# HGRN heads of a decoder trunk: the output norm in two halves, the last late projection's finish behind the keys' copies, and two weight sums of the feed-forward passage moved back

## The chip, the cores and the metric

The kernel runs on one core of a Trainium2 chip. The metric is the device time of one execution in microseconds (us); the median of several runs is compared. Where the text gives positions ("at 511 us"), they are counted from the start of the span of the profiled execution.

## What is computed

One layer of an autoregressive decoder, sequence 1024, width 1024, batch 1, all in fp32:

```
h <- h + W_out [ HGRN2 | dilated-window attention mixture | RWKV-7 ](W_in rmsnorm(h))
h <- h + gated MLP (width 2816) with causal depthwise conv (width 3) on rmsnorm(h)
h <- h + sigmoid(rmsnorm(h) W_g) * (p W_p)
...
final RMSNorm
```

The change is in the HGRN2 part (four heads, key and value width 128) and in the first half of the MLP. Of HGRN2, the part that matters here is its end, after the recurrence `S_t = diag(f_t) S_{t-1} + (1 - f_t) i_t^T, o_t = S_t^T q_t`:

```
o = o * lax.rsqrt(jnp.mean(o * o, axis=-1, keepdims=True) + NORM_EPS)      # per position and head, over 128
o = o.reshape(B_, S_, HG_WIDTH) * gnorm_g * jax.nn.silu(g_raw)
```

## The kernel before

Every dense product of fp32 numbers is made of three products of rounded parts: x = xh + xl, w = whi + wlo, and xh whi + xl whi + xh wlo is summed in PSUM (lines L137, L139, L141). ScalarE (ACT) makes the high parts, whi at L114 and xh at L160; VectorE (DVE) or GpSimd (POOL) makes the low parts, wlo at L116 and xl at L162. TensorE is PE.

The phases are: norm of x; RWKV with most of the projections by W_in; then the stretch that this change touches, from about 430 to 570 us: the four HGRN heads, the window attention, the last projections by W_in and the first tiles of W_out; then the rest of W_out, the MLP, the per-layer input and the final norm.

The stretch is written as generators that are advanced in turn by an order string: `A` is head 0 and then head 2, `B` head 1 and then head 3, `C` the attention (`swa`), `F` the late projections (`project_late`, in the order ... 18, 22, 23). Each `yield` is a place where another generator goes on. A scheduler then puts the instructions of every engine in one order. `tc.issue_after(x)` tells it that what is written inside must come later in the order than x; it adds no wait of its own.

One head, `hgrn_head`, goes: gates and decays on VectorE and GpSimd (names zl, hT, hk, qt); scores of chunks (hsc, masked into hS); transposes of the values (PE `vt`, L1043, copied to `hV` by ACT, L1044) and of the keys (`vt`, L1049, copied to `hkt` by ACT, L1050); the states (`hkv` in PSUM, `hst`); the outputs (`hpo`, L1083 and L1085). Then comes its end, L1086 to L1104: ACT copies the two halves of the output to `ho` (hf = 0 and then hf = 1, 128x512 each); ACT squares all of it (`hsq`, 128x1024); VectorE sums the squares by position (`hss`, 128x8) and applies mean and epsilon; GpSimd raises to -1/2 (`hrs`, 128x8); VectorE multiplies `ho` by it (L1097); PE transposes the two halves (`vt`, L1103); and VectorE multiplies by gain and gate (L1104). `o_split` then makes the two parts of the result for the product with W_out, whose PSUM tiles are `dp`.

In `project_late`, each projection is made in two halves of 128x512 (PSUM tile `zp`), and each half is finished at once: VectorE scales it (L320), ACT takes the sigmoid (`zst`, L457), VectorE multiplies (L459), and the queue of SP stores it to DRAM (L477), from where a head loads it back (`zl`, L488). For the last one, 23, this is the gate of head 3.

PSUM: a pool of four banks of 128x512 (`mx`) serves zp, vt, hsc, hkv, hpo and attention's tiles (swt, swo, swd) in turn. Attention's scores are `swq`; its probabilities lg, transposed by PE into swt and copied to pT.

In the first half of the MLP, weights and activations are combined by a seven-product scheme (p1 to p7) in the "passage" over the first units, at about 655 to 690 us. `sums` makes sums of weights of a unit on VectorE (L1448, L1450, L1451). The `y` of a unit is the last sum into V (L1510); PE writes into that PSUM tile again after it.

Of the kernel before, what the change touches and what calls it, by code (L numbers as in the profile page):

```python
# [22 lines left out]
NFF = 22  # L23
EPS = 1e-6
# [5 lines left out]
PC_LB, PC_GN, PC_MU = 32, 36, 40  # L30
# [59 lines left out]
class Trunk:  # L90
# [370 lines left out]
    def project_late(self, js):  # L461


        nc = self.nc
        for j in js:
            w = self.load_w(self.a["w_in"][j])
            t = self.keep.tile([P, T], F32, tag="zst", name=self.nm("zst"), bufs=2)
            d = self.zpool.tile([P, T], F32, tag=f"z{j}", name=f"z{j}")
            kind = (j - 8) % 4 if j < 24 else 2
            turn = j < 24 and kind < 3  # L470
            for hf in (0, 1):
                ps = self.mxp.tile([P, HT], F32, tag="mx", name=self.nm("zp"))
                self.dense({hf: ps}, w, self.X, ND, halves=(hf,))
                dst = slice((hf ^ turn) * HT, ((hf ^ turn) + 1) * HT)
                r = self.R[:, hf * HT:(hf + 1) * HT]
                self.finish(kind, t[:, dst], *((ps[:, ::-1], r[:, ::-1]) if turn and hf else (ps, r)))
                nc.sync.dma_start(d[:, dst], t[:, dst])  # L477
                if hf:
                    self.z[j] = d
                yield  # L480
        self.O = self.xall()
        for k in self.done:
            self.o_split(k)
            yield
# [469 lines left out]
    def hgrn_head(self, h):  # L954
        nc, mxp, par, spool = self.nc, self.mxp, self.par, self.spool
        j0 = 8 + 4 * h

        def view(t, off, *dims):
            return bass.AP(t.tensor, t.offset + off, [t.ap[0], *dims])

        f = self.zload(j0, self.slot)
# [77 lines left out]
        V = self.slot("hV")  # L1039
        for hf in (0, 1):  # L1040
            pt = mxp.tile([P, HT], F32, tag="mx", name=self.nm("vt"))
# [3 lines left out]
        kt = self.slot("hkt")  # L1045
        for hf in (0, 1):
            pt = mxp.tile([P, HT], F32, tag="mx", name=self.nm("vt"))
            for c in range(4):
                nc.tensor.transpose(pt[:, c * P:(c + 1) * P], k[:, hf * HT + c * P:hf * HT + (c + 1) * P], self.ident)  # L1049
            nc.scalar.copy(kt[:, hf * HT:(hf + 1) * HT], pt)  # L1050
        yield
        st = self.slot("hst")

        def at(cc, swap=False):
            c = (4 + cc if cc < 4 else 7 - cc) ^ (4 if swap else 0)
            return slice(c * P, (c + 1) * P)

        for hf in (0, 1):
# [6 lines left out]
            for c in range(4):  # L1065
# [3 lines left out]
                dst = st[:, (cc + 1) * P:(cc + 2) * P]  # L1069
# [5 lines left out]
                                                   ALU.mult, ALU.add)  # L1075
        yield
        o = self.slot("ho")
        for hf in (0, 1):
            po = mxp.tile([P, 4, P], F32, tag="mx", name=self.nm("hpo"))
            for c in range(4):  # L1080
                cc = 7 - c if hf == 0 else c
                s = at(cc)
                nc.tensor.matmul(po[:, c, :], S[:, s], V[:, s], start=True, stop=cc == 0)  # L1083
                if cc:
                    nc.tensor.matmul(po[:, c, :], qt[:, s], st[:, cc * P:(cc + 1) * P], start=False, stop=True)  # L1085
            nc.scalar.copy(o[:, hf * HT:(hf + 1) * HT], po.rearrange("p c v -> p (c v)"))  # L1086
        yield
        oa = self.zload(j0 + 3, self.slot)
        sq = self.slot("hsq")
        nc.scalar.activation(sq, o, AF.Square)  # L1090
        ss = spool.tile([P, 8], F32, tag="hss", name=self.nm("hss"))
        nc.vector.tensor_reduce(ss, sq.rearrange("p (c v) -> p c v", v=P), AX.X, ALU.add)
        nc.vector.tensor_scalar(ss, ss, 1.0 / P, EPS, ALU.mult, ALU.add)
        rs = spool.tile([P, 8], F32, tag="hrs", name=self.nm("hrs"))
        nc.gpsimd.tensor_tensor(rs, ss, self.mhalf[:, :8], ALU.pow)
        o3 = o.rearrange("p (c v) -> p c v", v=P)
        nc.vector.tensor_tensor(o3, o3, rs.unsqueeze(2).broadcast_to([P, 8, P]), ALU.mult)  # L1097
        yield
        for hf in (0, 1):
            sl = slice((1 - hf) * HT, (2 - hf) * HT)  # L1100
            pt = mxp.tile([P, HT], F32, tag="mx", name=self.nm("vt"))
            for c in range(4):
                nc.tensor.transpose(pt[:, c * P:(c + 1) * P], o3[:, hf * 4 + c, :], self.ident)  # L1103
            nc.vector.scalar_tensor_tensor(oa[:, sl], pt if hf else pt[:, ::-1], par[:, PC_GN + h:PC_GN + h + 1], oa[:, sl], ALU.mult, ALU.mult)  # L1104
        self.o[h] = oa
        self.dump(f"o{h}", oa)
        self.o_split(h)
# [324 lines left out]
    def phase_up(self):  # L1432
        nc, par, ep, cv, TX = self.nc, self.par, self.ep, self.cv, self.TX
        V, G = nc.vector, nc.gpsimd
# [9 lines left out]
        def sums(d):  # L1444
            a11, a12 = d["raw"][:, :HT], d["raw"][:, HT:]
            a21, a22 = d["rav"][:, :HT], d["rav"][:, HT:]
            s7 = ep.tile([P, HT], F32, tag="s7", name=self.nm("s7"), bufs=1)
            V.tensor_tensor(s7, a11, a21, ALU.add)  # L1448
            s6 = ep.tile([P, HT], F32, tag="s6", name=self.nm("s6"), bufs=2)
            V.tensor_tensor(s6, s7, a22, ALU.add)  # L1450
            V.tensor_tensor(a21, a21, a22, ALU.add)  # L1451
            d["s"] = {"3": s6, "4": a22, "5": a21, "6": s6, "7": s7, "2": a12}

        def w(d, n):
# [7 lines left out]
        def unit(d, prev):  # L1462
            f = d["f"]
# [8 lines left out]
            if prev:  # L1472
                ws["4"] = w(prev, "4")
            sums(d)
            for n in "652" if new else "65":
                ws[n] = w(d, n)
# [30 lines left out]
            x = cv.tile([P, HT], F32, tag="x", name=self.nm("x"), bufs=1)  # L1507
            d["x"] = V.tensor_tensor(x, d["e"], d["G"][:, HT:], ALU.add).ins
            self.mul((d["V"][:, :HT], ws["7"], TX["p7"], False))
            V.tensor_tensor(d["V"][:, HT:], x, d["V"][:, :HT], ALU.add)  # L1510

        def conv(d, part):
            f = d["f"]
# [35 lines left out]
        for d in self.units:  # L1549
            unit(d, prev)  # L1550
            prev = d
# [308 lines left out]
```

## Time and profile before

| | |
|---|---|
| median of 3 runs | 1404.72 us (1404.64 to 1406.29) |
| profiled execution: time | 1404.77 us |
| its span | 1403.0 us |
| mean granted clock of TensorE | 0.994 |
| PE busy | 1375.7 us, 98% of the span |
| DVE, ACT, POOL busy | 76%, 44%, 28% |

An entry of the profile such as `511.21 1.06 PE L1049 MATMUL vt<-cst,hk ... x4 [2.44 <-ACT hV L1044]` means: at 511.21 us four transposes that write vt began on TensorE; the engine had stood still for 2.44 us before, until ACT's instruction that writes hV, line 1044, was done. Line numbers are those of the kernel before; behind `issue_after` and the new code they are five to sixteen higher in the kernel after.

### The profile page before, as it was taken

Reading aid. Unit: us, or ns where it says so; the run is one execution under the profiler, and the core shown is the slowest. Engines: PE = TensorE matmul, PEld = TensorE weight load, DVE = VectorE, ACT = ScalarE, POOL = GpSimd, SP = SyncE. Lnnn points to the kernel's source line nnn. Section 1 sums busy time; section 2 is a strip of 40 time slices with the busy share of each in tenths; the row PEclk is TensorE's granted clock in tenths of the full one; section 3 lists DMA queues with packets and bytes.
Section 4 is the critical chain, followed back from the end, with each engine's and each line's share of the span. In section 5 each row is a group of like instructions: output and inputs, shape, how many; then the busy total and the mean of one; then the engine's idle time right before and its main releaser. Section 6 shows DMA issues by size and latency. Waiting matters only on the chain.

```text
span 1403.0 us, 22344 instructions
## 1 busy us (share of the span) xinstructions
PE 1375.7 (98%) x8644; PEld 1116.5 (80%) x8644; DVE 1063.7 (76%) x1613; ACT 611.8 (44%) x1049; POOL 395.5 (28%) x287
## 2 busy tenths in 40 slices
PE   9999999999999999999999999999999999999997
PEld 6878777877878768788788888888888888888886
DVE  7696456835667796468889888888988799777685
ACT  7522323133255584255544343444344444455542
POOL 5411012101222242221345454545453000002342
PEclk9999999999999999999999999999999999999998
DMA  6123111321622212653232332332324963441443
GB/s 224 61 83 104 64 61 47 100 73 62 225 83 99 91 61 71 253 180 125 94 127 98 113 103 90 102 105 98 114 98 166 351 217 106 127 143 45 136 138 140
DMA packets 80122, 167.61 MB, mean 119 GB/s; under 512 B 19984, under 2 KB 22288, under 8 KB 80016
## 3 DMA queue, kind: packets, MB, share of 16 engines
q1 hardware_dynamic: 66784, 147.05, 31.3%
q10 hardware_dynamic: 12224, 15.47, 3.2%
q0 software_dynamic: 1008, 3.67, 0.7%
q8 instruction: 68, 1.11, 0.3%
q14 instruction: 38, 0.31, 0.1%
HBM read 119.76 MB, written 46.40 MB: 118 GB/s over the span
## 4 chain that ended last, share of the span: by engine, by line
PE 78%; DVE 8%; issue 8%; ACT 3%; POOL 3%; DMA 1%; SPq 0%; POOLq 0%; ACTq 0%; DVEq 0%
PE bg L1338 17%; PE bv L1338 13%; PE bv L1639 7%; PE bg L1639 7%; PE dp L137 7%; PE dp L139 7%; PE dp L141 7%; PE swq L1169 1%; DVE ig L584 1%; PE hsc L1015 1%; PE zp L137 1%; DVE xl L409 1%; PE zp L141 1%; PE zp L139 1%; PE swo L1209 1%
## 5 line engine op out<-in xcount | busy, mean ns | idle before, releaser
L137 PE MATMUL dp<-xh,whi 128*128 128x512 f32 x544 | 186.9, 406 | 1.2 <-DVE r L502 0.7
L139 PE MATMUL dp<-xl,whi 128*128 128x512 f32 x544 | 180.5, 394 | 0.6 <-DVE xl L409 0.5
L141 PE MATMUL dp<-xh,wlo 128*128 128x512 f32 x544 | 179.7, 392 | 0.0
L116 POOL TENSOR_TENSOR wlo<-wraw,whi 128x512 fp32r<-128x512 f32 x60 | 84.5, 1410 | 264.9 <-ACT whi L114 226.8
L116 POOL TENSOR_TENSOR wlo<-raw,whi 128x512 fp32r<-128x512 f32 x84 | 135.0, 1626 | 75.9 <-ACT whi L114 75.9
L114 ACT CAST whi<-wraw 128x512 fp32r<-128x512 f32 x120 | 72.9, 618 | 158.0 <-PE dp L139 103.0
L1338 PE MATMUL bg<-t,whi 128*128 128x512 f32 x352 | 133.4, 389 | 0.0
L139 PEld LDWEIGHTS dp<-xl,whi 128*128 128x128 f32 x544 | 102.3, 188 | 24.6 <-DVE xl L409 2.5
L141 PEld LDWEIGHTS dp<-xh,wlo 128*128 128x128 f32 x544 | 102.2, 188 | 23.8 <-issue 2.0
L137 PEld LDWEIGHTS dp<-xh,whi 128*128 128x128 f32 x544 | 98.8, 189 | 26.0 <-issue 3.9
L116 POOL TENSOR_TENSOR wlo<-s,whi 128x512 fp32r<-128x512 f32 x44 | 64.5, 1466 | 168.6 <-ACT whi L114 168.6
L1639 PE MATMUL bg<-t,whi 128*128 128x512 f32 x308 | 95.2, 390 | 0.0
L1639 PE MATMUL bv<-t,whi 128*128 128x512 f32 x308 | 94.8, 389 | 0.0
L114 ACT CAST whi<-raw 128x512 fp32r<-128x512 f32 x88 | 52.7, 620 | 93.7 <-issue 48.5
L114 ACT CAST whi<-s 128x512 fp32r<-128x512 f32 x66 | 38.9, 620 | 120.2 <-PE bg L1338 112.8
L1338 PEld LDWEIGHTS bg<-t,whi 128*128 128x128 f32 x352 | 66.1, 188 | 13.7
L190 POOL TENSOR_TENSOR rst<-rst,mhalf 128x4 f32<-128x4 f32 (+1 forms) x9 | 10.2, 1134 | 234.0 <-DVE rst L186 218.0
L1635 ACT CAST t<-t 128x512 fp32r<-128x512 f32 x77 | 47.8, 622 | 45.8 <-PE bv L1639 32.7
L1338 PE MATMUL bg<-t,wlo 128*128 128x512 f32 x176 | 67.5, 389 | 0.0
L1639 PEld LDWEIGHTS bv<-t,whi 128*128 128x128 f32 x308 | 57.8, 188 | 12.0
L1639 PEld LDWEIGHTS bg<-t,whi 128*128 128x128 f32 x308 | 57.8, 188 | 11.9
L116 DVE TENSOR_TENSOR wlo<-wraw,whi 128x512 fp32r<-128x512 f32 x60 | 48.2, 807 | 20.7 <-ACT whi L114 18.5
(417 smaller groups left out, 3423.6 us busy)
## 6 DMA issues: line engine op xcount, KB each, us to landing
raw<-in_ffn_up_dram SPq DMA_DIRECT2D x44, 512.0 KB, 3.5
wraw<-in_w_in_dram SPq DMA_DIRECT2D x28, 512.0 KB, 3.4
z<-zst SPq DMA_DIRECT2D x18, 512.0 KB, 2.9
gb<-ct SPq DMA_DIRECT2D x33, 256.0 KB, 2.3
t<-gb SPq DMA_DIRECT2D x33, 256.0 KB, 2.7
t<-gt SPq DMA_DIRECT2D x33, 256.0 KB, 2.7
zl<-z SPq DMA_DIRECT2D x16, 512.0 KB, 4.4
wraw<-in_ple_gate_dram SPq DMA_DIRECT2D x16, 512.0 KB, 3.4
```

The source lines that it names most:

```text
L114: self.cast = nc.scalar.copy(hi, src).ins
L116: eng.tensor_tensor(lo, src, hi.bitcast(F32), ALU.subtract)
L137: nc.tensor.matmul(ps[hf], wh, xh[hf], start=first, stop=False)
L139: nc.tensor.matmul(ps[hf], wh, xl[hf], start=False, stop=False)
L141: self.step = nc.tensor.matmul(ps[hf], wl, xh[hf], start=False, stop=last).ins
L409: nc.vector.scalar_tensor_tensor(lo, x, g[:, k:k + 1], hi.bitcast(F32), ALU.mult, ALU.subtract)
L584: nc.vector.reciprocal(ig[:, hf * HT:(hf + 1) * HT], gam[:, hf * HT:(hf + 1) * HT])
L1015: nc.tensor.matmul(sc[g:g + 64, c, :], ks[:, c * P + g:c * P + g + 64], x, start=True, stop=True)
L1169: m = nc.tensor.matmul(pq[h][:, b:b + w], d["q"][hs, qb * P:nk], d["k"][hs, b:b + w], start=True, stop=True)
L1338: nc.tensor.matmul(ps, w[part == 2][:, s], X[k][part == 1], start=start and k == part == 0, stop=k == 3 and part == 2, skip_group_check=no ...
L1635: nc.scalar.copy(xh, x)
L1639: nc.tensor.matmul(ps[m], wt[part == 2][:, m * P:(m + 1) * P], (xh, xl)[part == 1], start=k == part == 0, stop=k == NK - 1 and part == 2)
```

## The change

1. `project_late`: the second half of the last projection (23) is finished behind a `yield`, and in the order behind the copies of the keys of a head (`self.keys`).
2. `hgrn_head`: the output halves are made in the order hf = 1, hf = 0. Each half is copied, squared, summed, and raised to -1/2 by itself; the copy of the second half comes behind the square of the first. Both multiplies (128x512 each) come behind the second half's mean; the multiplies by gain and gate come behind both.
3. `sums` of the MLP: for unit 2, two of the three sums come behind the y of unit 0.

Per head this is one ACT instruction more, three VectorE instructions and one GpSimd instruction more. No matmul and no transfer is added.

```
@@ project_late
                 r = self.R[:, hf * HT:(hf + 1) * HT]
-                self.finish(kind, t[:, dst], ...)
+                with ExitStack() as order:
+                    if hf and j == js[-1]:
+                        yield
+                        order.enter_context(self.tc.issue_after(self.keys))
+                    self.finish(kind, t[:, dst], ...)
                 nc.sync.dma_start(d[:, dst], t[:, dst])
                 if hf:
                     self.z[j] = d
-                yield
+                if not (hf and j == js[-1]):
+                    yield
@@ hgrn_head
-            nc.scalar.copy(kt[:, hf * HT:(hf + 1) * HT], pt)
+            self.keys = nc.scalar.copy(kt[:, hf * HT:(hf + 1) * HT], pt).ins
...
-        for hf in (0, 1):
+        squared = None
+        for hf in (1, 0):
             po = mxp.tile([P, 4, P], F32, tag="mx", name=self.nm("hpo"))
...
-            nc.scalar.copy(o[:, hf * HT:(hf + 1) * HT], po.rearrange("p c v -> p (c v)"))
-        yield
-        oa = self.zload(j0 + 3, self.slot)
-        sq = self.slot("hsq")
-        nc.scalar.activation(sq, o, AF.Square)
-        ss = spool.tile([P, 8], F32, tag="hss", name=self.nm("hss"))
-        nc.vector.tensor_reduce(ss, sq.rearrange("p (c v) -> p c v", v=P), AX.X, ALU.add)
-        nc.vector.tensor_scalar(ss, ss, 1.0 / P, EPS, ALU.mult, ALU.add)
-        rs = spool.tile([P, 8], F32, tag="hrs", name=self.nm("hrs"))
-        nc.gpsimd.tensor_tensor(rs, ss, self.mhalf[:, :8], ALU.pow)
-        o3 = o.rearrange("p (c v) -> p c v", v=P)
-        nc.vector.tensor_tensor(o3, o3, rs.unsqueeze(2).broadcast_to([P, 8, P]), ALU.mult)
-        yield
-        for hf in (0, 1):
+            s, c = slice(hf * HT, (hf + 1) * HT), slice(4 * hf, 4 * hf + 4)
+            if hf:
+                oa = self.zload(j0 + 3, self.slot)
+                sq = self.slot("hsq")
+                ss, rs = [spool.tile([P, 8], F32, tag=n, name=self.nm(n)) for n in ("hss", "hrs")]
+                o3 = o.rearrange("p (c v) -> p c v", v=P)
+            with ExitStack() as order:
+                if squared is not None:
+                    order.enter_context(self.tc.issue_after(squared))
+                nc.scalar.copy(o[:, s], po.rearrange("p c v -> p (c v)"))
+            squared = nc.scalar.activation(sq[:, s], o[:, s], AF.Square).ins
+            nc.vector.tensor_reduce(ss[:, c], sq[:, s].rearrange("p (c v) -> p c v", v=P), AX.X, ALU.add)
+            m = nc.vector.tensor_scalar(ss[:, c], ss[:, c], 1.0 / P, EPS, ALU.mult, ALU.add)
+            nc.gpsimd.tensor_tensor(rs[:, c], ss[:, c], self.mhalf[:, :4], ALU.pow)
+        yield
+        with self.tc.issue_after(m.ins):
+            for c in (slice(4, 8), slice(0, 4)):
+                m = nc.vector.tensor_tensor(o3[:, c], o3[:, c], rs[:, c].unsqueeze(2).broadcast_to([P, 4, P]), ALU.mult)
+        yield
+        for hf in (1, 0):
...
-            nc.vector.scalar_tensor_tensor(oa[:, sl], ...)
+            with self.tc.issue_after(m.ins):
+                nc.vector.scalar_tensor_tensor(oa[:, sl], ...)
@@ sums
-            V.tensor_tensor(s6, s7, a22, ALU.add)
-            V.tensor_tensor(a21, a21, a22, ALU.add)
+            with ExitStack() as order:
+                if d["f"] == 2:
+                    order.enter_context(self.tc.issue_after(self.units[0]["y"]))
+                V.tensor_tensor(s6, s7, a22, ALU.add)
+                V.tensor_tensor(a21, a21, a22, ALU.add)
...
-            V.tensor_tensor(d["V"][:, HT:], x, d["V"][:, :HT], ALU.add)
+            d["y"] = V.tensor_tensor(d["V"][:, HT:], x, d["V"][:, :HT], ALU.add).ins
```

How the order of the engines moves, at three places. First ScalarE where head 1's values and keys are copied and projection 23 is finished (hV and hkt are the copies, zst the sigmoid, lg attention's exponentials, pT and ob attention's copies, xh and whi splits). Before:

```order
377 L457 ACT_TABLE_LOAD
378 L457 ACTIVATE zst_5011<-zp_5201 128x512
379 L1044 COPY hV_5230<-vt_5231 128x512
380 L1044 COPY hV_5230<-vt_5237 128x512
381 L1050 COPY hkt_5243<-vt_5244 128x512
382 L1050 COPY hkt_5243<-vt_5250 128x512
383 L1181 ACT_TABLE_LOAD
384 L1181 ACTIVATE lg_5313,sden_5121<-lg_5313,sden_5121 128x768
385 L1181 ACTIVATE lg_5316,sden_5121<-lg_5316,sden_5121 128x768
```

After:

```order
380 L160 CAST xh_5295<-oc_3420 128x512
381 L1049 COPY hV_5236<-vt_5237 128x512
382 L1049 COPY hV_5236<-vt_5243 128x512
383 L1055 COPY hkt_5249<-vt_5250 128x512
384 L1055 COPY hkt_5249<-vt_5256 128x512
385 L457 ACT_TABLE_LOAD
386 L457 ACTIVATE zst_5021<-zp_5211 128x512
387 L1223 COPY ob_4979<-swo_5329 128x128
388 L1209 COPY pT_5340<-swt_5341 128x512
389 L1007 COPY ks_5389<-hk_5114 128x2x64x4
390 L1209 COPY pT_5350<-swt_5351 128x512
391 L1194 ACT_TABLE_LOAD
```

Table load and sigmoid now stand behind the four copies; the two exponentials of 128x768 have gone ahead of the copies (rows 371 and 373 of the order after), and the second table load stands behind attention's copies.

Second, VectorE at the end of head 0 (hss sums of squares, ho the norm's multiply, pT and hS, qt as above). Before:

```order
551 L1092 TENSOR_REDUCE hss_4549<-hsq_4547 128x8
552 L1196 COPY pT_4515<-swt_4522 128x384
553 L1196 COPY pT_4527<-swt_4534 128x384
554 L1093 TENSOR_SCALAR hss_4549<-hss_4549 128x8
555 L1017 COPY_PREDICATED hS_4231<-cmask,hsc_4555 128x4x64
556 L1097 TENSOR_TENSOR ho_4454<-ho_4454,hrs_4552 128x1024
557 L1028 TENSOR_TENSOR qt_4169<-qt_4169,hT_4233 128x2x32x8
```

After:

```order
549 L1103 TENSOR_REDUCE hss_4466<-hsq_4465 128x4
550 L1104 TENSOR_SCALAR hss_4466<-hss_4466 128x4
551 L1022 COPY_PREDICATED hS_4231<-cmask,hsc_4487 128x4x64
552 L1033 TENSOR_TENSOR qt_4169<-qt_4169,hT_4233 128x2x64x4
553 L1103 TENSOR_REDUCE hss_4466<-hsq_4465 128x4
554 L1104 TENSOR_SCALAR hss_4466<-hss_4466 128x4
555 L1109 TENSOR_TENSOR ho_4454<-ho_4454,hrs_4467 128x512
556 L1209 COPY pT_4528<-swt_4535 128x384
557 L1109 TENSOR_TENSOR ho_4454<-ho_4454,hrs_4467 128x512
558 L1209 COPY pT_4540<-swt_4547 128x384
559 L1022 COPY_PREDICATED hS_4231<-cmask,hsc_4560 128x4x64
```

The first half's sum stands four rows ahead of the second's, and attention's copies stand between and behind the two multiplies.

Third, VectorE in the MLP's passage (s and raw are sums of weights; bv is V, its row at L1510 before and at L1526 after is the y of unit 0). Before:

```order
847 L1459 TENSOR_TENSOR s_1216_7052<-s_1216_7052,raw_6565 128x512
848 L116 TENSOR_TENSOR wlo_7065<-s_1215_7050,whi_7063 128x512
849 L1448 TENSOR_TENSOR s_1236_7163<-raw_7146,raw_7148 128x512
850 L1450 TENSOR_TENSOR s_1237_7165<-s_1236_7163,raw_7148 128x512
851 L1510 TENSOR_TENSOR bv_6999<-x_7026,bv_6999 128x512
```

After:

```order
853 L116 TENSOR_TENSOR wlo_7085<-s_1215_7070,whi_7083 128x512
854 L1461 TENSOR_TENSOR s_1236_7183<-raw_7166,raw_7168 128x512
855 L1526 TENSOR_TENSOR bv_7019<-x_7046,bv_7019 128x512
856 L1466 TENSOR_TENSOR s_1237_7185<-s_1236_7183,raw_7168 128x512
857 L1467 TENSOR_TENSOR raw_7168<-raw_7168 128x512
```

One sum, that of s_1237, which stood ahead of y, now stands behind it.

More of the change, by code (lines that the diff above doesn't have):

```diff
@@ L475, in project_late @@
                 r = self.R[:, hf * HT:(hf + 1) * HT]
-                self.finish(kind, t[:, dst], *((ps[:, ::-1], r[:, ::-1]) if turn and hf else (ps, r)))
+                with ExitStack() as order:
+                    if hf and j == js[-1]:
+                        yield
+                        order.enter_context(self.tc.issue_after(self.keys))
+                    self.finish(kind, t[:, dst], *((ps[:, ::-1], r[:, ::-1]) if turn and hf else (ps, r)))
                 nc.sync.dma_start(d[:, dst], t[:, dst])
@@ L1103, in hgrn_head @@
                 nc.tensor.transpose(pt[:, c * P:(c + 1) * P], o3[:, hf * 4 + c, :], self.ident)
-            nc.vector.scalar_tensor_tensor(oa[:, sl], pt if hf else pt[:, ::-1], par[:, PC_GN + h:PC_GN + h + 1], oa[:, sl], ALU.mult, ALU.mult)
+            with self.tc.issue_after(m.ins):
+                nc.vector.scalar_tensor_tensor(oa[:, sl], pt if hf else pt[:, ::-1], par[:, PC_GN + h:PC_GN + h + 1], oa[:, sl], ALU.mult, ALU.mult)
         self.o[h] = oa
```

## The prediction

> **What bounds the kernel now.** I read the page's first part, then stretches of time, then TensorE's own timeline for the places where it stands still, and last the queues of the engines that it waits for there. First the page:
>
> ```profile
> span 1403.0 us, 22344 instructions
> PE 1375.7 (98%) x8644; PEld 1116.5 (80%) x8644; DVE 1063.7 (76%) x1613; ACT 611.8 (44%) x1049; POOL 395.5 (28%) x287
> ```
>
> TensorE (PE) is busy for 98% of the span; this change adds and removes no matmul, so it can win only stalls of PE and time at a low clock. The stretches (columns: length, busy time of PE, PEld, DVE, ACT, POOL, granted clock, DMA share, GB/s) say where those are:
>
> ```profile
> 430.00:570.00 140.00, 132.41 (x1264) 107.62 (x1261) 103.69 (x208) 74.92 (x145) 39.78 (x32) 0.99 0.29 97
> 570.00:655.00 85.00, 85.00 (x387) 70.43 (x387) 52.87 (x80) 38.36 (x63) 19.31 (x15) 1.00 0.51 179
> 692.00:1280.00 588.00, 587.82 (x2598) 486.51 (x2596) 505.83 (x611) 261.69 (x386) 187.94 (x121) 1.00 0.40 131
> ...
> 512.00:518.00 6.00, 6.00 (x54) 4.36 (x53) 5.27 (x15) 5.71 (x11) 1.49 (x1) 0.77 0.43 131
> 560.00:565.00 5.00, 3.20 (x18) 2.48 (x18) 2.88 (x4) 1.24 (x2) 1.44 (x2) 1.00 0.56 207
> 688.00:692.00 4.00, 2.79 (x13) 1.98 (x12) 3.77 (x4) 0.82 (x2) 2.29 (x2) 1.00 0.29 112
> ```
>
> From 430 to 570 us, where the HGRN heads end, PE loses 140.00 - 132.41 = 7.59 us; from 570 to 655 it is full, and from 692 to 1280 it loses 0.18 of 588 us. What is won ahead of a full stretch is therefore carried to the end. In 512 to 518 PE is full but the clock is 0.77: against full clock that hides 6.00 x (1 - 0.77) = 1.4 us. TensorE's own rows (start, length, operation, count, then the idle time before it and who ended it) name the stalls:
>
> ```profile
> 450.22 0.69 PE L1015 MATMUL hsc<-qt,ks 128*64 128x64 f32 x16 [0.59 <-ACT pT L1196]
> 451.45 0.50 PE L137 MATMUL zp<-xh,whi 128*128 128x512 f32 x1 [0.55 <-DVE pT L1196]
> ...
> 507.21 1.56 PE L1169 MATMUL swq<-zl,zl 64*128 64x512 f32 x8
> 511.21 1.06 PE L1049 MATMUL vt<-cst,hk 128*128 128x128 f32 x4 [2.44 <-ACT hV L1044]
> ...
> 536.73 0.52 PE L1103 MATMUL vt<-cst,ho 128*128 128x128 f32 x3 [1.17 <-DVE ho L1097]
> ...
> 561.99 1.06 PE L1103 MATMUL vt<-cst,ho 128*128 128x128 f32 x8 [1.80 <-DVE ho L1097]
> ...
> 690.15 0.50 PE L1338 MATMUL bv<-tp4h,whi 128*128 128x512 f32 x1 [1.21 <-DVE bv L1510]
> ```
>
> These six waits are 7.76 us, and each stands at a place that the change touches.
>
> **Part 1: the last late projection's finish goes behind the keys' copies.** The queues ahead of the 2.44 us wait:
>
> ```profile
> 507.01 0.61 ACT L160 CAST xh<-oc 128x512 fp32r<-128x512 f32 x1
> 507.65 1.28 ACT L457 ACT_TABLE_LOAD   x1
> 510.09 0.60 ACT L457 ACTIVATE zst<-zp 128x512 f32<-128x512 f32 x1 [1.16 <-DVE zp L320]
> 510.58 1.07 ACT L1044 COPY hV<-vt 128x512 f32<-128x512 f32 x2
> ...
> 507.69 1.75 DVE L116 TENSOR_TENSOR wlo<-wraw,whi 128x512 fp32r<-128x512 f32 x1
> 509.37 0.69 DVE L320 TENSOR_TENSOR zp<-zp,rstd 128x512 f32<-128x512 f32 x1
> 510.72 0.69 DVE L459 TENSOR_TENSOR zst<-zst,zp 128x512 f32<-128x512 f32 x1 [0.66 <-ACT zst L457]
> ```
>
> ACT works in order: the values' copies (hV) stand behind the sigmoid, the sigmoid behind VectorE's scale, and the scale behind a weight split of 1.75. With sigmoid and table load behind the keys' copies, hV can start when the cast ends, 507.01 + 0.61, and is done by about 508.7; PE's swq work lasts until 507.21 + 1.56 = 508.77. So the 2.44 goes, and with it, I hold, the 1.4 us of low clock: 3.8. The same work must run later. Table load and sigmoid (1.28 + 0.60 = 1.88) now lie ahead of attention's copies of ob and pT, the multiply of 0.69 ahead of its mask work on VectorE, and the projection's PSUM bank (one of four) is held until that multiply instead of to 511.4. Attention scores and an early share of its softmax move ahead, into the earlier gap. Stepping the new queue of PE against those durations I find two to four small waits of 0.3 to 0.7; I charge 1.2. Bounds: nothing is charged (-3.8) and the whole 1.88 + 0.69 shows as one wait (-1.2). Taken: -2.6. The store of the last z moves back with its multiply, to about 515; the load of z (at 519.69, below) is later still. The number of table loads stays at two around here, now both behind the keys' copies.
>
> ```profile
> 519.69 9.71 SPq L488 DMA_DIRECT2D zl<-z  x2
> ...
> 555.70 2.03 SPq L1347 DMA_DIRECT2D raw<-in_ffn_up_dram  x4
> ...
> 569.86 0.69 DVE L1448 TENSOR_TENSOR s<-raw,raw 128x512 f32<-128x512 f32 x1
> ```
>
> The rule that speaks against the clock part is in the Trainium skill, "TensorE: Matmul & The Clock Gate", Part 1: the clock falls to half after about one idle window of 3.4 us, and the window runs freely. By it a stall of 2.44 us alone need not cost any clock, and the 1.4 us might stay; the sum would then be 1.4 smaller. Against it stands that the fall comes directly behind the longest stall, while 1.80 and 1.21 us elsewhere left the clock at 1.00.
>
> **Part 2: the norm by halves, four heads.** Prices of the old steps (lowest, median, highest in ns) and the end of head 3:
>
> ```profile
> L1090 ACT ACTIVATE hsq<-ho x4: 1056/1060/1102, 443.2 to 556.3; 128x1024 f32<-128x1024 f32 x4
> L1092 DVE TENSOR_REDUCE hss<-hsq x4: 1212/1220/1223, 444.2 to 557.4; 128x8 f32<-128x1024 f32 x4
> L1095 POOL TENSOR_TENSOR hrs<-hss,mhalf x4: 1637/1837/2011, 446.5 to 558.9; 128x8 f32<-128x8 f32 x4
> L1097 DVE TENSOR_TENSOR ho<-ho,hrs x4: 1224/1226/1226, 448.2 to 560.6; 128x1024 f32<-128x1024 f32 x4
> L190 POOL TENSOR_TENSOR rst<-rst,mhalf x9: 697/1017/1508, 37.5 to 1394.8; 128x4 f32<-128x4 f32 x7, 128x2 f32<-128x2 f32 x2
> ...
> 555.66 0.59 ACT L1086 COPY ho<-hpo 128x512 f32<-128x512 f32 x1 [1.67 <-PE hpo L1085]
> ...
> 558.70 0.17 DVE L1093 TENSOR_SCALAR hss<-hss 128x8 f32<-128x8 f32 x1
> ```
>
> For the half that ends last, square, reduce and multiply are half as wide; a VectorE operation of 128x512 takes 0.68 to 0.69 and an ACT copy of that size 0.59. The pow of 128x4 isn't in this place; nearest is L190 (mostly 128x4): 0.70 to 1.51, I take 1.02. The chain behind the last copy shrinks by (1.06 - 0.6) + (1.22 - 0.68) + (1.84 - 1.02) + (1.23 - 0.69) = 2.4 us; with the pow's ends 1.9 to 2.7. In head 3 the multiply then ends near 559.5 and PE's last transposes could start near 560, not at 561.99. Not all of it is PE's: the order puts both transposes a little ahead of the remaining output matmuls of that stretch, so PE still meets about 0.9, and the tail behind it (gate multiply, split of the last o into xh and xl, then the matmuls that need them) about 0.4; 1.80 becomes 1.3 less some 0.2 that the tail cost before: -0.7. Head 2: transposes 0.8 earlier than 536.73, but two output matmuls that ran ahead of them now run behind: -0.5. Bounds for both: all of 1.17 + 1.80 goes (-3.0), or nothing (0). Taken: -1.2.
>
> Head 0:
>
> ```profile
> 448.25 1.23 DVE L1097 TENSOR_TENSOR ho<-ho,hrs 128x1024 f32<-128x1024 f32 x1 [1.42 <-POOL hrs L1095]
> ...
> 450.71 0.69 DVE L1196 COPY pT<-swt 128x512 f32<-128x512 f32 x1
> ```
>
> Here VectorE stands 1.42 before the multiply, and PE then waits 0.59 and 0.55 for what is queued behind it (the copy pT last). With the halves the multiply is done by about 447, so both waits can go: bounds -1.14 and 0; taken -1.0. Head 1 ends with PE busy and gives nothing. Per head the change adds a square, three VectorE operations and a pow: VectorE 2 x 0.68 - 1.22 = 0.14 twice (reduce, multiply) and one 0.17, 0.45 in all; ACT 2 x 0.59 - 1.06 = 0.12; POOL 2 x 1.02 - 1.84 = 0.2. They lie in VectorE's 36 and ACT's 65 idle us of this stretch, so nothing; were that cover gone, at most 4 x 0.45 = 1.8. The gate's load is issued between the halves; in head 0 that puts it ahead of a store and a w_out load on SP. The four raw loads (2 MB) now wait for the last transposes, about 560 instead of 555.70, nearer to the eight loads of h; their first reader was at 569.86 (the row above), ten us behind that: nothing.
>
> **Part 3: two sums of unit 2 behind unit 0's y.** VectorE's queue at the 1.21 us wait, and the next unit's:
>
> ```profile
> 687.82 1.66 DVE L1450 TENSOR_TENSOR s<-s,raw 128x512 f32<-128x512 f32 x1
> 689.41 0.68 DVE L1510 TENSOR_TENSOR bv<-x,bv 128x512 f32<-128x512 f32 x1
> ...
> 691.08 0.69 DVE L1489 TENSOR_TENSOR bg<-bg,v 128x512 f32<-128x512 f32 x1
> ...
> 704.03 1.27 DVE L1521 SCALAR_TENSOR_TENSOR ct<-bv,ncw,ct 128x1022 f32<-128x1022 f32 x1
> 705.22 0.68 DVE L1510 TENSOR_TENSOR bv<-x,bv 128x512 f32<-128x512 f32 x1
> ...
> 706.62 0.39 PE L1338 MATMUL bv<-tp4h,whi 128*128 128x512 f32 x1
> ```
>
> Without the 1.66 ahead of it y (L1510) starts at 687.82 and is done at 688.50; PE reaches its reader at 690.15 - 1.21 = 688.94. The wait goes. But the next unit gives some back: VectorE does the same work up to 691.8, so its y still ends at 705.90, while PE would be at the reader at 706.62 - 1.21 = 705.41. About 0.5 returns. Bounds: -1.21 and -0.7; taken -0.8.
>
> **Sum.** 2.6 + 1.2 + 1.0 + 0.8 = 5.6. The profiled execution took 1404.77 (span 1403.0 and 1.8 around it), 0.05 above the median of the runs, so the forecast is 1399.1.
>
> **Rivals.** (a) The clock stays low, because the fall belongs to the row of transposes and short attention matmuls and not to the wait: 5.6 - 1.4 = 4.2, 1400.5. For it: only one such fall is to be seen. Against: head 3's transposes kept 1.00. (The rule of the Trainium skill, "TensorE: Matmul & The Clock Gate", Part 1, leaves room for this case.) (b) The waits only move: PE's idle time is set by ACT and VectorE, which do not get less work; if half the stall at 511 and most of heads 2 and 3 come back at the next attention or output matmul, 1.2 + 0.8 is left: 1402.7. For it: the small waits I found; against: both engines have room. (c) All goes: 7.76 + 1.4 = 9.2, less the 0.5 at the next unit and 0.7 for the tail: 1396.8. (d) Slower: the late finish holds its PSUM bank while it queues behind the keys' copies. If its multiply ends only about 515.3 and the next tile in turn needs that bank at 510.5, PE waits 4.8, at a clock loss in proportion (1.4 x 4.8 / 2.44 = 2.8): 7.6 instead of 3.8, net +3.8, with the other parts' 3.0 gained: 1405.5. It decides from a new wait of about 4.3 us, which needs PE to use all four banks at once. Against it: before, the 54 matmuls of 512 to 518 ran without any wait. (e) The ordering changes nothing: the order of the engines shows that it does; 1404.7.
>
> **Chances.** Forecast (1398 to 1400.2) 0.50, (a) 0.13, (c) 0.15, (b) 0.15, (d) 0.05, (e) 0.02. A change under 0.2%, 2.8 us, can't be told from none: (b) is at 2.0 and mostly inside, (d) half inside. Range 1396.2 to 1402.6. Faster 0.82, same 0.15, slower 0.03.
>
> **What would show it.** After: the vt behind hV without a stall over 0.5 and a granted clock near 1.00 behind it; hV copies near 508 ahead of the sigmoid; pow rows near 1.0 us, eight of them; the last transposes with under 1 us of wait; y of unit 0 done before 689 in today's time, and a wait near 0.5 at the next unit's bv. Wrong if the clock still falls, if a stall over 1 us stands at attention's swt or swq between 510 and 520, or if the pow of half width costs as much as the whole.

## The result, and the profile after

The changed kernel is slower: 1413.69 us (median of 8, 1408.55 to 1415.17) against 1406.07 us (8 runs, 1404.64 to 1406.87), a ratio of 1.0048 with an interval of 1.0039 to 1.0057. The forecast was 1399.1, with a range to 1402.6. The eight times lie in two groups, three at 1408.6 to 1409.2 and five at 1413.6 to 1415.2; the profiled execution is of the lower group.

Two corrections to the text ahead. By the traces, the values' and keys' copies near 510 us are those of head 2 (they were called head 1's), and the scan beside them (hT, hk, hS) is head 3's. And `issue_after(x)` orders only those instructions of its block that run on x's engine: in part 1 that is the sigmoid and its table load. VectorE's scale of the late half ran at 508.83, ahead of the last copy of the keys at 511.76.

The page of the changed kernel, and its table of whom TensorE waited for (total, times, longest):

```profile
span 1406.8 us, 22358 instructions
...
PE 1377.7 (98%) x8644; PEld 1116.5 (79%) x8644; DVE 1069.4 (76%) x1625; ACT 612.6 (44%) x1053; POOL 396.9 (28%) x291
...
PE swt L1208 <- DVE hS L1022: 3.1, 1, 3.1
...
PE vt L1115 <- DVE ho L1109: 1.7, 2, 1.0
...
PE hsc L1020 <- DVE qt L1033: 1.6, 3, 0.7
...
PE bg L1351 <- DVE x L1524: 0.7, 1, 0.7
...
PE vt L1115 <- DVE zst L459: 0.5, 1, 0.5
PE swt L1208 <- DVE pT L1209: 0.5, 1, 0.5
PE bv L1351 <- DVE ct L1537: 0.4, 1, 0.4
```

Every wait that the change aimed at is gone or smaller: 2.44 at the keys' transposes, 0.59 and 0.55 at head 0, 1.21 in the passage, and 1.17 + 1.80 became 1.7. In their place stands one of 3.1 us at attention's transposes (swt), and several of 0.3 to 0.7. TensorE there, with the scores of the 1024-key turn (swq) behind the stall; below it the same scores in the kernel before:

```profile
517.12 0.33 PE L1208 MATMUL swt<-cst,lg 128*128 128x128 f32 x1 [3.12 <-DVE hS L1022]
517.90 1.33 PE L1208 MATMUL swt<-cst,lg 128*128 128x128 f32 x5 [0.45 <-DVE pT L1209]
519.02 1.92 PE L1069 MATMUL hkv<-hV,hkt 128*128 128x128 f32 x8
520.87 2.17 PE L1182 MATMUL swq<-zl,zl 64*128 64x512 f32 x4
522.97 0.49 PE L1069 MATMUL hkv<-hV,hkt 128*128 128x128 f32 x2
523.39 1.98 PE L1182 MATMUL swq<-zl,zl 64*128 64x512 f32 x4
```

```profile
521.05 1.99 PE L1169 MATMUL swq<-zl,zl 64*128 64x512 f32 x8
```

This shows a second loss, which no table of waits shows, since TensorE is busy in it. Before, the eight rows of both heads took 1.99 us. Now two state matmuls (hkv) stand between the heads, and the four rows of one head alone take 1.98 to 2.17: 4.15 in all. The turn of 768 keys is torn apart likewise (1.55 + 1.55, before 1.56 for both).

VectorE ahead of the stall, and ScalarE:

```profile
508.83 0.69 DVE L320 TENSOR_TENSOR zp<-zp,rstd 128x512 f32<-128x512 f32 x1
509.43 1.16 DVE L1038 TENSOR_TENSOR hT<-zl 128x512 f32<-128x512 f32 x1
510.69 1.57 DVE L1031 TENSOR_TENSOR hk<-hk,hT 128x512 f32<-128x512 f32 x1
512.19 4.52 DVE L1038 TENSOR_TENSOR hT<-hT 128x256 f32<-128x256 f32 x6
516.64 0.43 DVE L1022 COPY_PREDICATED hS<-cmask,hsc 128x256 f32<-128x256 uint8 x1
...
518.78 0.68 DVE L459 TENSOR_TENSOR zst<-zst,zp 128x512 f32<-128x512 f32 x1
```

```profile
509.16 1.07 ACT L1049 COPY hV<-vt 128x512 f32<-128x512 f32 x2
...
511.76 0.59 ACT L1055 COPY hkt<-vt 128x512 f32<-128x512 f32 x1 [1.03 <-PE vt L1054]
512.36 1.28 ACT L457 ACT_TABLE_LOAD   x1
513.66 0.60 ACT L457 ACTIVATE zst<-zp 128x512 f32<-128x512 f32 x1
```

ScalarE does what was forecast: the copies come ahead of sigmoid and table load. But on VectorE head 3's whole scan, six products of 4.52 us, and hk before it with 1.57, now stand ahead of the masked copy hS. That copy empties the PSUM bank of hsc, which the next swt needs. The late half's own bank is held until its multiply ends at 519.46.

TensorE's time from one row's start to the next, added up by tile from 424 us to the first product of the per-layer input (643.55 before, 647.34 after), gives this for the profiled executions: idle +0.5, scores +2.7, hkv +1.2, all else -0.8, together +3.6 us. Of hkv, scores and swt a part is low clock: half clock stood from 517.9 to 521.3, one stretch of 3.41 us, as there was one from 511.3 to 514.7 before. The idle time and the clock of this execution thus hardly changed; it lost by the scores, and by hkv, which now ran at half clock. The upper group loses elsewhere, as the runs below show.

### The profile page after: what moved, and what is told of

Same layout as the page of the kernel before. It is cut to its first block, busy times and chain, and to the rows that moved or that the text cites. A ratio compares the mean times of both kernels' runs of the same rounds, so it can differ in the third digit from the quotient of the medians.

```text
span 1406.8 us, 22358 instructions
## 1 busy us (share of the span) xinstructions
PE 1377.7 (98%) x8644; PEld 1116.5 (79%) x8644; DVE 1069.4 (76%) x1625; ACT 612.6 (44%) x1053; POOL 396.9 (28%) x291
## 3 DMA queue, kind: packets, MB, share of 16 engines
q8 instruction: 68, 1.11, 0.3%
## 4 chain that ended last, share of the span: by engine, by line
PE 76%; DVE 9%; issue 8%; ACT 2%; POOL 2%; DMA 1%; SPq 0%; POOLq 0%; ACTq 0%; DVEq 0%
PE bg L1351 16%; PE bv L1351 12%; PE bv L1655 7%; PE bg L1655 7%; PE dp L137 7%; PE dp L139 7%; PE dp L141 7%; PE swq L1182 1%; DVE ig L589 1%; PE zp L137 1%; DVE xl L409 1%; PE hsc L1020 1%; PE zp L139 1%; PE zp L141 1%; PE swt L1208 1%
```

## The experiments

### Each part alone

`e1`: part 1 on the kernel before. `e2`: part 2 alone. `e3`: part 3 alone. `e4`: the changed kernel again.

> The kernel before with part 1 alone (late finish behind the keys' copies). Theory L (part 1 holds one of four PSUM banks from about 505 to 519 us while head 3's scan stands on VectorE ahead of the hS copy that frees the next bank; PE stalls about 3 us and the clock falls): the 2.44 wait at hV goes, another of 2 to 4 us comes behind it, the granted clock still falls to 0.5 for at least one window, and the time is 2 to 8 us above the kernel before. Theory N (the loss comes from the norm's extra instructions): part 1 alone gains what was predicted for it, 2 to 4 us, about 1403.

> The kernel before with part 2 alone (norm by halves in four heads). Theory L: 1 to 2.5 us faster than the kernel before, since the waits of 0.59 and 0.55 at head 0 and most of 1.80 and 1.17 at heads 3 and 2 go, and only some 0.5 to 1 comes back as small waits. Theory N: 3 to 8 us slower, with new waits of PE on VectorE at the heads.

> The kernel before with part 3 alone (two sums of unit 2 behind unit 0's y). The 1.21 us wait at 690 goes; waits of about 0.4 and 0.7 come at 705 to 725 as in the changed kernel. Both theories: within 0.5 us of the kernel before, so the predicted 0.8 is not there. If those later waits do not come, 1.0 us faster.

> The changed kernel unaltered, for its times beside the others on this chip and for another trace. Its eight times lie in two groups, about 1409 and about 1414. Theory C (where the free window of the clock lies against the 3.1 us stall decides how many windows of half clock follow): a run of the upper group shows the same waits as the run seen, and one to four more windows of 3.4 us at half clock. Rival Q (the upper group has other waits, of DMA or engines): its sum of PE waits is 3 to 5 us larger and its clock the same.

| run | median us | lowest to highest | ratio to before (95%) |
|---|---|---|---|
| e1 part 1 | 1410.09 | 1408.20 to 1411.37 | 1.0031 (1.0019 to 1.0043) |
| e2 part 2 | 1406.09 | 1404.52 to 1408.23 | 1.0006 (0.9997 to 1.0015) |
| e3 part 3 | 1406.07 | 1405.17 to 1407.64 | 1.0005 (0.9996 to 1.0013) |
| e4 the change | 1415.09 | 1414.43 to 1415.50 | 1.0067 (1.0054 to 1.0080) |

Part 1 loses by itself, as theory L said, and its stall is the longest of all, above L's 2 to 4; part 2 has no gain, and shows two stalls that the heads do not explain. TensorE in e1, and then in e2:

```profile
517.69 0.47 PE L1200 MATMUL swt<-cst,lg 128*128 128x128 f32 x1 [5.29 <-DVE hS L1022]
```

```profile
512.11 0.66 PE L1049 MATMUL vt<-cst,hk 128*128 128x128 f32 x4 [0.44 <-ACT hV L1044]
516.34 0.77 PE L1203 MATMUL swt<-cst,lg 128*128 128x128 f32 x5 [1.19 <-DVE hS L1017]
518.63 3.35 PE L1064 MATMUL hkv<-hV,hkt 128*128 128x128 f32 x14 [1.53 <-DVE pT L1204]
```

So all but 0.44 of the 2.44 us wait goes by part 2 alone as well: the halves shift the order of all that follows. In its place come 1.19 and 1.53, and two windows of half clock (6.83 us). Neither theory had e2 right: L expected a gain of 1 to 2.5, N a loss of 3 to 8. Part 3 behaves as both had it: nothing. Neither e1 nor e2 separates the two heads' scores of 1024 keys (eight rows stand together in both), so that loss belongs to the parts together. In e4 the waits are those of the run seen before (3.12 at swt, 0.39 instead of 0.45 behind it), but half clock lasts 17.07 us, five windows. At half speed that costs 8.5 us instead of 1.7, and the span is 6.6 us longer (1413.4 against 1406.8). Both signs of theory C are there, the same waits and four more windows, the most that it allowed; Q falls. The stretches of e4:

```profile
521.00:525.00 4.00, 4.00 (x8) 1.54 (x6) 2.25 (x6) 2.95 (x5) 0.00 (x0) 0.50 0.61 201
525.00:530.00 5.00, 5.00 (x8) 1.92 (x8) 0.00 (x0) 0.00 (x0) 0.00 (x0) 0.50 0.00 0
530.00:535.00 5.00, 5.00 (x56) 4.61 (x56) 3.15 (x7) 0.62 (x1) 0.00 (x0) 0.59 0.00 0
```

TensorE is busy all the time and still runs at 0.50.

### VectorE's order, and the bank

`e5` is the changed kernel, `e7` the norm alone and `e12` the late finish alone, each with this edit:

```
+                m = nc.vector.copy_predicated(D, mask(l), sc)
+                first = m.ins if l == 1 else first
...
+            with ExitStack() as order:
+                if h == 3 and 1 < l < 7:
+                    order.enter_context(self.tc.issue_after(first))
                 nc.vector.tensor_tensor(Tn, T3[:, :, 0], T3[:, :, 1], ALU.mult)
```

`e6` is the changed kernel with the late half's bank emptied at once:

```
                     if hf and j == js[-1]:
+                        u = self.spool.tile([P, HT], F32, tag="sqt", name=self.nm("zu"), bufs=2)
+                        nc.vector.tensor_tensor(u, ps, r, ALU.mult)
                         yield
                         order.enter_context(self.tc.issue_after(self.keys))
+                        nc.scalar.activation(t[:, dst], u, AF.Sigmoid)
+                        nc.vector.tensor_tensor(t[:, dst], t[:, dst], u, ALU.mult)
```

> The changed kernel, with VectorE's chain of small products of head 3 (hT, levels 2 to 6) put behind the hS copy of level 1; the late finish still holds its PSUM bank to about 518. Theory L (the 3.1 us stall is that bank wait, and the half clock follows the stall): the stall at swt goes to under 1 us, the clock does not fall to half near 517, and the time drops by 4.5 to 10 us against the changed kernel's 1409 to 1415, to about 1404 to 1406; the attention scores of 1024 keys still take about 4 us, since their order on PE is the same. Rival H (holding the bank is enough, whatever the order): the stall stays at 2 us or more, and the time at 1408 or above.

> The changed kernel, with the late half scaled from PSUM into an SBUF tile at once (its bank free at about 510), sigmoid and multiply behind the keys' copies from there. The order then has hS ahead of hT, and the four score matmuls of 1024 keys next to each other. Theory L: no stall over 1.2 us between 505 and 530, no half clock there, scores of 1024 keys in 2.0 us: 3 to 6 us faster than the kernel before, 1400 to 1403. Rival H2 (a wait of some 3 us in this stretch is given by VectorE's work and only changes its place): a new stall of 2 us or more elsewhere from 505 to 530, the clock falls, and the time is at 1405 or above.

> The kernel before with the norm by halves alone, and the same chain of head 3 behind its hS copy. In the run with the norm alone two stalls of 1.2 and 1.5 us and two windows of half clock took the place of the 2.44. Theory L: both stalls shrink to under 0.7, the clock holds, and the time is 2 to 5 us below the kernel before, about 1401 to 1404. Rival N (the norm's own extra work costs): at 1405.5 or above.

> The kernel before with the late finish alone (which stalled 5.3 us at swt and ran at 1410) and head 3's chain behind its hS copy. Theory L: the stall shrinks to under 2 us, at most one half-clock window, 1402 to 1406. Rival H (holding the bank until after the keys' copies suffices): the stall stays above 3 us and the time above 1408.

| run | median us | lowest to highest | ratio to before (95%) |
|---|---|---|---|
| e5 the change, scan behind hS | 1406.26 | 1404.86 to 1408.17 | 1.0006 (0.9997 to 1.0014) |
| e6 the change, bank free | 1406.53 | 1404.52 to 1408.40 | 1.0007 (0.9998 to 1.0016) |
| e7 norm, scan behind hS | 1403.75 | 1402.88 to 1404.52 | 0.9985 (0.9976 to 0.9994) |
| e12 late finish, scan behind hS | 1406.81 | 1405.16 to 1407.47 | 1.0006 (0.9998 to 1.0015) |

With one order of VectorE changed, the change as a whole goes from 1409 to 1415 down to 1406.3, and the late finish alone from 1410.1 to 1406.8. The norm alone gains 2.3 us against e2, and its spread shrinks to 1.6 us. TensorE's waits in e5, in e7 and in e12:

```profile
516.72 0.77 PE L1212 MATMUL swt<-cst,lg 128*128 128x128 f32 x5 [1.84 <-DVE pT L1213]
```

```profile
515.56 0.84 PE L1207 MATMUL swt<-cst,lg 128*128 128x128 f32 x5 [0.56 <-DVE hS L1017]
517.00 1.83 PE L1068 MATMUL hkv<-hV,hkt 128*128 128x128 f32 x14 [0.60 <-DVE pT L1208]
```

```profile
515.74 0.33 PE L1204 MATMUL swt<-cst,lg 128*128 128x128 f32 x1 [3.31 <-DVE hS L1022]
```

In e5 the wait on hS is gone, as theory L said, but 1.84 remains at the copy pT, above L's bound of 1; the time is at the upper end of L's range, and no half clock shows in the profile, as L said. In e7 the stalls are as expected. In e12 the scan stands behind hS, yet VectorE does hk and two mask operations (0.94 each) first, and 3.31 remains. That wait is on rival H's side (above 3), the single window of half clock on L's, and the time lies between the two: moving the scan alone does not free the banks in time. What moves with the edits is VectorE's queue, 3 to 5 us of which must be done ahead of the copies that free the banks.

In e6 the bank of the late half is free, hS goes at 511.99, and the wait stands at pT, behind hk (VectorE in e6, then TensorE):

```profile
513.67 1.75 DVE L1038 TENSOR_TENSOR hk<-hk,hT 128x512 f32<-128x512 f32 x1
515.34 0.28 DVE L1216 COPY pT<-swt 128x128 f32<-128x128 f32 x1
```

```profile
515.67 0.33 PE L1215 MATMUL swt<-cst,lg 128*128 128x128 f32 x1 [2.54 <-DVE pT L1216]
```

So rival H2 holds for the place of the wait and for the time, though the clock of the profiled execution did not fall. Theory L's gain of 3 to 6 us is not there. How much of the 3.1 us belongs to the held bank alone is not settled: e6 changes VectorE's order as well.

### Scores of two heads

`e8` is the kernel before with the loops over heads and over blocks of keys exchanged in the score matmuls. `e9` (the change), `e10` (e5) and `e11` (e7) keep the two heads next to each other, by putting the first score matmul behind those that had come in between; e13 and e14 do it for one turn each:

```
+        self.BEHIND = {(1, 5): lambda: self.turned, (1, 7): lambda: self.states}
...
+                        if (d["p"], qb) in self.BEHIND:
+                            late.enter_context(self.tc.issue_after(self.BEHIND[d["p"], qb]()))
                         m = nc.tensor.matmul(pq[h][:, b:b + w], ...)
```

(`turned` is the last transpose of a turn's probabilities, `states` the last matmul of hkv; in e11 only the entry for turn 5 is there.)

> The kernel before, with the score matmuls of two heads (64 rows of the array each) one head after the other instead of in turn, for all turns with over 512 keys (eight of them). Theory P (in turn, two such matmuls of different array halves run at once, and the changed kernel lost about 2.1 us because its 1024-key scores were no longer in turn): each of these turns takes close to twice as long, 0.7 to 2.1 us more, and the kernel is 6 to 13 us slower. Rival: the 4.15 us of the changed kernel came from the low clock and a bank, the turns keep 1.3 to 2.0 us, and the time stays within 1 us.

> The changed kernel, with the score matmuls of the two heads next to each other again for the turns of 768 and of 1024 keys (they stand behind the transposes and the state matmuls that had come between them). In the changed kernel each head's four rows took the time of both: 1.55 + 1.55 for 768 keys (1.56 before) and 1.98 + 1.98 for 1024 (1.99 before). Theory A (apart from each other, the heads lose the overlap of the array's two halves): 3 to 4 us less than the changed kernel at the same number of half-clock windows, the VectorE order and its stall of 3 us as before. Rival: the scores were only waiting in another place, and PE stalls by as much instead: the same time as the changed kernel, 1409 to 1415.

> The same two turns kept together, on the changed kernel with head 3's chain behind its hS copy (1406.26). Theory A: 3 to 4 us less, 1402 to 1403.5. Rival: a stall of 1.8 us at swt stays and others come: 1405 or above.

> The kernel before with the norm by halves, head 3's chain behind its hS copy (1403.75), and the turn of 768 keys kept together. Theory A: 1.0 to 1.6 us less, about 1402.3, the fastest so far. Rival: no less than 1403.5.

| run | median us | lowest to highest | ratio to before (95%) |
|---|---|---|---|
| e8 heads one after the other | 1405.93 | 1404.84 to 1407.23 | 1.0002 (0.9993 to 1.0011) |
| e9 the change, heads together | 1407.26 | 1405.85 to 1407.96 | 1.0010 (1.0001 to 1.0019) |
| e10 e5, heads together | 1403.68 | 1402.65 to 1405.07 | 0.9988 (0.9979 to 0.9997) |
| e11 e7, heads together | 1402.97 | 1402.15 to 1403.63 | 0.9983 (0.9974 to 0.9991) |

Theory P falls as it stood: in e8 the 1024-key turn still takes 1.99 us, and the time is the same, as its rival said. Whether the heads' matmuls alternate does not matter there. The rival's cause, low clock and a bank, is not it either: what costs is another matmul between them, as e9 and e10 show. The scores in e8, and in e9:

```profile
521.21 1.99 PE L1169 MATMUL swq<-zl,zl 64*128 64x512 f32 x8
```

```profile
498.94 2.37 PE L1186 MATMUL swq<-zl,zl 64*128 64x512 f32 x8
524.51 1.99 PE L1186 MATMUL swq<-zl,zl 64*128 64x512 f32 x8
```

With the heads together, 4 us of 1024-key scores become 1.99, and 3.10 of 768-key scores 2.37. By rows that is 1.97 + 0.73 = 2.7 us; from e5 to e10 the median falls by 2.58, and from e7 to e11, where only the second was torn, by 0.78. Theory A holds for the cause and is above its true size (3 to 4 us forecast for e10, 1.0 to 1.6 for e11): the 768-key turn keeps 0.8 us more than its 1.56, for a reason that stays open, and a new wait of 0.29 stands ahead of it. e9 falls by far more than 2.7, since its upper group is gone. e11 is the fastest kernel here, faster than before by 0.09 to 0.26%.

### Why the half clock lasts

> The changed kernel with the heads' scores kept together for the turn of 768 keys alone; the 1024-key scores stay apart, right behind the 3.1 us stall. Theory K (matmuls on half of the array, one after the other, are too little work to bring the clock back, so half clock lasts while they run): some executions with three to five windows of half clock, times in two groups or all high, up to 1412 to 1414, median at least 2 us above the kernel with both turns together (1407.26). Rival (the number of windows is chance of the free window alone): the spread as with both together, at most two windows, 1407 to 1410.

> The changed kernel with the heads' scores kept together for the turn of 1024 keys alone; the 768-key scores stay apart, ahead of the stall at full clock. Theory K: at most two windows of half clock, 1406 to 1409.5, some 0.7 us above the kernel with both together (that turn took 2.37 us there with 0.29 of wait, and 3.1 apart). Rival: the upper group at 1412 to 1414 is there.

| run | median us | lowest to highest | ratio to before (95%) |
|---|---|---|---|
| e13 only 768 keys together | 1413.47 | 1409.41 to 1414.04 | 1.0052 (1.0039 to 1.0065) |
| e14 only 1024 keys together | 1407.50 | 1406.88 to 1408.49 | 1.0013 (1.0004 to 1.0022) |

The stall is the same in both, 3.12 us. With the 1024-key heads apart behind it, half clock lasted 13.65 us in the profiled run and four of five times are above 1413; with them together it lasted 3.41 us, and no time is above 1408.5. The scores in e13, and one stretch of e14:

```profile
517.91 1.92 PE L1069 MATMUL hkv<-hV,hkt 128*128 128x128 f32 x8
519.76 3.78 PE L1186 MATMUL swq<-zl,zl 64*128 64x512 f32 x4
523.47 0.79 PE L1069 MATMUL hkv<-hV,hkt 128*128 128x128 f32 x2
524.19 3.78 PE L1186 MATMUL swq<-zl,zl 64*128 64x512 f32 x4
```

```profile
521.00:525.00 4.00, 4.00 (x48) 3.24 (x49) 3.17 (x9) 3.58 (x6) 0.00 (x0) 0.91 0.64 201
```

Theory K holds: in e13 matmuls on 64 rows of the array, one head at a time, keep TensorE "busy" for 7.6 us, with only 0.79 us of hkv between them, and the clock does not come back. They make the upper group possible.

Which group an execution falls into goes with where the clock is judged. Within an execution the half-clock stretches begin whole multiples of 3.413 us apart (in the kernel before at 9.57, 511.33 and 1391.97), so every trace gives its own grid of windows, also where the clock did not fall in this stretch. One window of e10's grid, and one each of those of e2, e12 and e13 (the second number is TensorE's busy time, the third from the end the clock):

```profile
514.17:517.58 3.41, 1.58 (x15) 1.34 (x14) 3.38 (x7) 2.19 (x5) 2.42 (x2) 1.00 0.44 154
514.42:517.83 3.41, 1.50 (x12) 1.02 (x10) 3.38 (x6) 2.05 (x5) 1.45 (x2) 1.00 0.60 213
516.55:519.96 3.41, 3.41 (x14) 1.82 (x11) 2.97 (x9) 0.54 (x3) 0.00 (x0) 0.50 0.20 77
524.68:528.10 3.42, 3.42 (x5) 0.88 (x5) 0.00 (x0) 0.00 (x0) 0.00 (x0) 0.50 0.00 0
```

In all sixteen traces, from 424 to 648 us, the clock fell behind every full-clock window in which TensorE stood idle for 1.92 us or more, and behind none with 1.83 or less. The lowest idle time with a fall is that of e2 above, where a stall of 1.19 and part of one of 1.53 lie in one window; the highest without one is that of e10, a single stall of 1.83. The stalls of 2.41 in e8 and 2.54 in e6 cost no clock because a window's edge cut them, into 1.33 and 1.08 and into 1.18 and 1.37. In e12's window the two heads' scores stand next to each other, and the clock was back at its end; behind e13's, where one head's scores fill it, it stayed at 0.50. In the lower group's trace the first window at half clock has 0.02 us of idle time and the clock came back; in e4 the rest of the stall lies in that window, 1.11 us, and the scores of one head follow. This is seen in these two traces; the other executions of the changed kernel have none.

## Why the prediction was wrong, step by step

- **Part 1, forecast -2.6.** The step that failed is the replay of the new order: "two to four small waits of 0.3 to 0.7". It took the bank behind hsc as free in time, and charged 1.2 us where one wait alone came to 3.12. The measured wait is 3.12 + 0.45: VectorE's scan of 4.52 and hk of 1.57 stand ahead of hS, while the late half holds its own bank. The upper bound was wrong too: it let a delay of the late finish show once, as 1.2 us of gain at worst, and had no row for work of another head that is drawn ahead on VectorE. e1 measured +4.35 us. The slower rival (d) had this place, the held bank and a wait of 4.8 us, at 1405.5 with a chance of 0.05; its point against itself, the 54 matmuls of 512 to 518 without a wait, was an argument about the old order.
- **The clock, forecast -1.4.** It was right that half clock follows idle time of TensorE, and not the kind of work ahead of it: e5 and e7, with 1.84 and 0.6 at most, show none in their profiles. But not every stall of that length costs it (2.44 did, 2.41 in e8 did not), which the prediction did not reckon with. The term was also a little small: the window before is 3.41 us long, 1.7 us and not 1.4. It was wrong that the stall goes. What was not thought of at all is the length: one window of 3.41 us or five, by where the windows lie and by the work behind the stall.
- **The order of the scores** had no term. The rows of the order were stepped for what waits, not for what runs beside what. It is worth 2.7 us in the changed kernel, as much as the largest forecast gain (2.6).
- **Part 2, forecast -1.2 and -1.0.** At the waits it aimed at it was about right: head 0's 0.59 and 0.55 are gone, head 3 has 0.96 and 0.33 where 0.9 and 0.4 were forecast, head 2 has 0.72 instead of 1.17. "Head 1 gives nothing" was too mild: 0.65 and 0.47 are new there, and the 768-key scores behind are torn (+0.8 to 1.5). Ahead of head 3's hsc, 0.19 and 0.73 stand where 0.43 stood. Added up, the waits at the heads fell from 4.85 to 4.21 us, a gain of 0.6 and not 2.2. With order and scores mended, e11 is 2.5 us faster than the kernel before (1402.97 against 1405.51). That this is close to 2.2 is luck: by the two traces the heads' waits give 0.3 of it; the wait of 2.44, which shrank to 1.57 in three pieces, gives 0.9, and the window of half clock that is gone 1.7, less 0.8 for the 768-key scores. These are the places of part 1.
- **Part 3, forecast -0.8.** The 1.21 went and 0.43 came back at the next unit, near the forecast 0.5, though behind the convolution's ct and not behind y; another 0.71 at that unit's x was missed:

```profile
709.22 0.47 PE L1351 MATMUL bv<-tp6h,whi 128*128 128x512 f32 x1 [0.43 <-DVE ct L1537]
...
724.08 0.50 PE L1351 MATMUL bg<-tp3h,whi 128*128 128x512 f32 x1 [0.71 <-DVE x L1524]
```

  Together 1.14 of 1.21: nothing is left, and e3 shows nothing.
- **Prices.** A square, a reduce and a multiply of half width cost what was taken (0.6, 0.68, 0.69). The pow of half width costs 1.2 in the median, inside its bounds and a little above the 1.02 taken:

```profile
L1105 POOL TENSOR_TENSOR hrs<-hss,mhalf x8: 1011/1206/1446, 442.7 to 561.8; 128x4 f32<-128x4 f32 x8
L1109 DVE TENSOR_TENSOR ho<-ho,hrs x8: 678/692/694, 444.8 to 563.2; 128x512 f32<-128x512 f32 x8
...
L1103 DVE TENSOR_REDUCE hss<-hsq x8: 671/686/687, 441.7 to 560.9; 128x4 f32<-128x512 f32 x8
...
L1102 ACT ACTIVATE hsq<-ho x8: 615/630/636, 441.0 to 560.2; 128x512 f32<-128x512 f32 x8
```

The half-clock stretches measured between 424 and 648 us are 3.41, 6.83, 13.65 and 17.07 us long, all multiples of 3.41. This agrees with the Trainium skill, "TensorE: Matmul & The Clock Gate", Part 1, by which the clock is judged in free windows of 3413 ns. It does not agree on what brings the clock back: by that page one busy window is enough, and here TensorE was busy for 5.00 of 5.00 us at 0.50 (e4), while most of its matmuls used half of the array's rows. Nor must a whole window be idle: 1.92 of 3.41 us were enough (e2).

## What to carry to other kernels

When one engine's wait is taken out of a planned order, read anew on every other engine which instruction frees the banks that the waiting engine needs next, and what now stands ahead of it; an ordering on one engine lets the planner pull other work forward on the rest. Step a changed matmul order for what runs beside what, and not for waits alone: heads on two halves of the array must stay next to each other. For the clock, count TensorE's idle time in windows of 3.41 us and not by single stalls: two short ones close together cost it as one long one does. Where such a stall can't be avoided, see that work on the whole array follows it, or the half clock outlasts the stall several times over.

## What the runs showed of the hardware that was not expected

Two score groups on different halves of the array run beside each other when nothing stands between them, whichever way they alternate (eight rows in 1.99 us), and take twice that when a full-array matmul does (1.98 each). After a stall, such matmuls of one head at a time left the clock at 0.50 through three windows without idle time (e4 and e13), although TensorE counts as busy; at full clock, 3.1 us of them in one window did not make it fall (the changed kernel, 521.3 to 524.7). The clock fell behind windows of 3.41 us with 1.92 us or more of idle time, and not behind those with 1.83 or less.
